# The opening norm of a two-block model: its inverse root alone on VectorE, its blocks scaled ahead of the shift, and the first mixer weights prepared between its blocks

## Chip, cores and metric

The kernel runs on one core of a Trainium2 chip. The metric is the device time of one execution in microseconds, the median over several runs. TensorE does the matmuls, VectorE (DVE in the views) and ScalarE (ACT) the elementwise work, GpSimd (POOL) some of it, and SyncE (SP) issues all the DMAs of weights and tables, in order.

## The reference

The input x is 256 tokens of 1024 features, all in float32. A first block of two layers is followed by a second block (gated linear attention, forgetting attention, cross-attention, a SwiGLU). Only the start of the first block matters here. In short:

```python
mod = (silu(c) @ ada_w[layer] + ada_b[layer])[:, None, :]
shift_m, scale_m, gate_m, shift_f, scale_f, gate_f = split(mod, 6)
h = rmsnorm(x, norm_g[layer, 0]) * (1.0 + scale_m) + shift_m
mix = mixer(h)                     # layer 0: convolution and retention; layer 1: S5
x = x + gate_m * mix
h = rmsnorm(x, norm_g[layer, 1]) * (1.0 + scale_f) + shift_f
x = x + gate_f * (square(relu(h @ w_fc1[layer])) @ w_fc2[layer])
```

The S5 mixer of layer 1 needs tables made from its parameters alone (complex exponentials and their powers, and per group of channels a matrix V and a matrix W). They don't depend on x, so the kernel makes them while the first layer runs.

## The kernel before

**Layout and weights.** Features lie on the partitions: x is eight blocks of 128 features by 256 tokens. Float32 is emulated: a weight piece of 1 MB (128 x 2048) is loaded by SP into a pool of four buffers, ScalarE makes its hi part (`hilo`, L314) and VectorE its lo part, the remainder (L315), in four quarters of 128x512. Each piece is then used in 48 matmuls of 128x256: hi by hi, hi by lo and lo by hi (`mm3`, L319 to L321). The activations are split into hi and lo as well.

**Modulation.** `ada(l, which)` makes 8 of a layer's 48 modulation columns: four pieces of 1 MB through the same four buffers, eight matmuls each (L439; the trace shows 16 records a piece), then a transposition on VectorE (L444) and the addition of the bias (L445). The first two calls make the scale and the shift of the first norm. All later ones are in a list (`Fill`) of which `step_piece` in the mixer takes some steps ahead of each weight piece (1.25 a piece on average).

**The norm.** `rms` squares x on ScalarE (L155), sums over the features on TensorE (L167), takes the inverse root on VectorE (`rsqrt`: eleven tiny operations, L344 to L349, behind L354) and spreads it over the partitions with TensorE (L369), into PSUM. `normed` then does for each of eight blocks: x times gain times root on VectorE (L397), the shift added on ScalarE, which gives hi (L398), and lo on VectorE (L399). The mixer's first weight pieces follow (`mixer0`, L497 on): value and gate of the convolution branch for j = 0 and 1 (`w_in` 0, 2, 1, 3), then tanh and the product (L518, L519), then the 31 taps of the convolution on VectorE, ScalarE and GpSimd.

**S5 preparation.** `s5_prep` (L739 to L835) is some 150 operations on VectorE and ScalarE (128x64 up to 128x576; complex products in `cmul`, L703 to L708). It is traced before the modulation. `s5_load(i)` loads the coefficients of group i (tile bc, L859), `s5_out(i)` makes the matrix V from them (L867, L871, L872, L881; for groups 0 to 2 on GpSimd), and `s5_tables` the rest: matmuls on V (L907), the matrix W on VectorE (L881, L921, L922), its transposition on TensorE (L928), copies on ScalarE (L929) and the stores to DRAM (Vd at L897, Wd at L932). `begin` starts groups 0 and 1 in the mixer; group 2 is started by `s5_tables` behind the first Wd store.

**Order.** The code is traced in one sequence; a scheduler then orders each engine's queue by a simulated time and a priority that falls with the place in the trace. `held(engines)` puts what is traced inside it behind the last instruction traced so far on these engines, `held_at(ends)` behind a given one, `later(n)` gives way to the next n instructions, and `after` puts steps of a fill behind an anchor on one engine. Each engine then works its queue strictly in that order.

## Time and profile before

| | |
|---|---|
| three runs | 1226.87, 1230.74, 1236.1 us |
| median | 1230.74 us |
| profiled execution, first to last instruction (span) | 1227.2 us |
| TensorE busy | 1169.7 us (95%) |
| VectorE busy | 891.7 us (73%) |
| ScalarE busy | 609.7 us (50%) |
| GpSimd busy | 106.1 us (9%) |

The span is measured from the first to the last instruction of one execution, and is what the profiled execution's own time is known by; it lies 0.3 us above the fastest run and 3.5 us below the median. TensorE is busy nearly everywhere, with two places of idle time in the first 210 us and one at 437 to 509 us. Times in the rows are microseconds from the span's start. Matmuls are pipelined, so the distance of two starts says what one costs, and its own duration is longer; the same holds for small operations of VectorE. The granted clock of TensorE (PEclk) is 1.00 at 2.4 GHz and 0.50 at 1.2 GHz.

### The profile page before, as it was taken

How to read it: one execution, taken by the hardware profiler on the slowest of the kernel's cores; microseconds unless marked ns; L12 is line 12 of the kernel's file. 1: busy time of each engine (PE TensorE's matmuls, PEld its weight loads, DVE VectorE, ACT ScalarE, POOL GpSimd, SP SyncE). 2: the span in 40 equal slices, each digit the busy share in tenths (PEclk: the TensorE clock that was granted, in tenths of full speed). 3: DMA queues.
4: the chain of work that ended last, by engine and by line, in shares of the span. 5: the costliest groups of instructions: out<-in, count | busy, mean ns of one | idle time of the engine just before them, and what ended most of it. 6: DMA issues, size and time to landing. Idle time of an engine off the chain costs nothing. (4 is left out here: it accounts for less than half of the span.)

```text
span 1227.2 us, 25417 instructions
## 1 busy us (share of the span) xinstructions
PE 1169.7 (95%) x10482; PEld 1109.3 (90%) x10482; DVE 891.7 (73%) x1821; ACT 609.7 (50%) x1202; POOL 106.1 (9%) x138
## 2 busy tenths in 40 slices
PE   6899897999999976899999999999999999999998
PEld 4698686999999964899999999999999999999998
DVE  7879888889888859767765656686667686665564
ACT  3577244655555542545544545573465545544441
POOL 0077321000000006200000000000000000000000
PEclk8899997999999977799999999999999999999999
DMA  9888886688888999554466655453443454555541
GB/s 341 340 311 327 297 294 212 238 265 282 297 287 267 300 249 309 216 172 171 169 243 212 233 174 172 164 172 104 151 159 138 172 168 148 194 179 177 194 155 60
DMA packets 69979, 267.29 MB, mean 218 GB/s; under 512 B 7380, under 2 KB 35428, under 8 KB 43240
## 3 DMA queue, kind: packets, MB, share of 16 engines
q1 hardware_dynamic: 69864, 265.68, 63.5%
q8 instruction: 82, 1.34, 0.4%
q14 instruction: 33, 0.27, 0.1%
HBM read 246.85 MB, written 18.81 MB: 216 GB/s over the span
## 5 line engine op out<-in xcount | busy, mean ns | idle before, releaser
L315 DVE TENSOR_TENSOR lo<-w,hi 128x512 fp32r<-128x512 f32 (+1 forms) x640 | 427.6, 712 | 147.7 <-ACT hi L314 147.1
L314 ACT ACTIVATE hi<-w 128x512 fp32r<-128x512 f32 (+1 forms) x640 | 358.4, 625 | 337.0 <-PE mm L320 118.8
L319 PE MATMUL mm<-h,hi 128*128 128x256 f32 x1328 | 379.7, 286 | 0.3 <-ACT h L398 0.3
L320 PE MATMUL mm<-h,hi 128*128 128x256 f32 x1328 | 377.7, 285 | 1.3 <-DVE h L399 1.1
L321 PE MATMUL mm<-h,lo 128*128 128x256 f32 x1328 | 378.6, 285 | 0.0
L319 PEld LDWEIGHTS mm<-h,hi 128*128 128x128 f32 x1328 | 254.7, 192 | 7.2 <-issue 3.4
L320 PEld LDWEIGHTS mm<-h,hi 128*128 128x128 f32 x1328 | 254.6, 192 | 2.8 <-DVE h L399 1.5
L321 PEld LDWEIGHTS mm<-h,lo 128*128 128x128 f32 x1328 | 254.5, 192 | 2.6 <-issue 1.6
L321 PE MATMUL at<-s,lo 128*128 128x256 f32 x720 | 204.4, 284 | 1.7 <-DVE lo L315 1.7
L319 PE MATMUL at<-s,hi 128*128 128x256 f32 x720 | 204.8, 284 | 0.0
L320 PE MATMUL at<-s,hi 128*128 128x256 f32 x720 | 204.1, 284 | 0.0
L321 PEld LDWEIGHTS at<-s,lo 128*128 128x128 f32 x720 | 137.9, 192 | 2.5 <-DVE lo L315 2.1
L319 PEld LDWEIGHTS at<-s,hi 128*128 128x128 f32 x720 | 138.0, 192 | 1.8 <-issue 1.4
L320 PEld LDWEIGHTS at<-s,hi 128*128 128x128 f32 x720 | 138.0, 192 | 0.6 <-issue 0.6
L439 PE MATMUL fa<-wa,crep 128*32 128x256 f32 x704 | 56.4, 428 | 7.0 <-DMA wa<-in_ada_dram 3.8
L537 POOL TENSOR_TENSOR s<-s,cv 128x256 f32<-128x256 f32 x60 | 49.9, 866 | 38.9 <-ACT cv L536 38.7
L439 PEld LDWEIGHTS fa<-wa,crep 128*32 128x32 f32 x704 | 23.0, 120 | 27.0 <-issue 6.4
L319 PE MATMUL fp<-h,hi 128*128 128x256 f32 x144 | 41.9, 291 | 0.7 <-ACT h L314 0.7
L320 PE MATMUL fp<-h,hi 128*128 128x256 f32 x144 | 41.8, 290 | 0.0
L321 PE MATMUL fp<-h,lo 128*128 128x256 f32 x144 | 41.6, 289 | 0.0
L929 ACT COPY Wt<-fp 128x512 f32<-128x512 f32 x32 | 18.6, 581 | 43.3 <-PE fp L928 39.9
L536 ACT ACTIVATE cv<-ap,s 128x256 f32<-128x256 f32 x60 | 29.5, 506 | 17.2 <-POOL s L537 16.4
(438 smaller groups left out, 1829.6 us busy)
## 6 DMA issues: line engine op xcount, KB each, us to landing
w<-in_fc_dram SPq DMA_DIRECT2D x64, 1024.0 KB, 5.1
wa<-in_ada_dram SPq DMA_DIRECT2D x44, 1024.0 KB, 6.5
w<-in_w_in_dram SPq DMA_DIRECT2D x38, 1024.0 KB, 4.9
w<-in_w_gate_dram SPq DMA_DIRECT2D x11, 1024.0 KB, 5.0
w<-in_w_up_dram SPq DMA_DIRECT2D x11, 1024.0 KB, 4.9
Vd<-V SPq DMA_DIRECT2D x16, 512.0 KB, 6.6
w<-in_w_out_dram SPq DMA_DIRECT2D x8, 1024.0 KB, 6.2
Wd<-Wt SPq DMA_DIRECT2D x16, 512.0 KB, 5.2
```

Of the source, the lines that this page charges most:

```text
L314: self.nc.scalar.activation(hi, h, AF.Copy)
L315: self.nc.vector.tensor_tensor(lo, h, hi.bitcast(F32), op=ALU.subtract)
L319: mm(ps, sh, mh, start=start, stop=False, skip_group_check=True)
L320: mm(ps, sh, ml, start=False, stop=False, skip_group_check=True)
L321: mm(ps, sl, mh, start=False, stop=stop, skip_group_check=True)
L439: nc.tensor.matmul(ps[32 * q:32 * q + 32], self.crep[:, 2 * k + k2], w[:, n:n + 256], start=k == 0 and k2 == 0, stop=k == 3 and k2 == 1, t ...
L536: nc.scalar.mul(t, src, w)
L537: nc.gpsimd.tensor_tensor(acc[:, ch], acc[:, ch], t, op=ALU.add)
L929: nc.scalar.copy(W[:, :, k], pt.rearrange("p (e x) -> p e x", e=4))
```

## The change

It has five parts.

1. The modulation is traced in front of most of the S5 preparation: the scale, three of the shift's four pieces, the root, then six of the eight blocks x times gain times root (`scaled`), and only then the shift's last piece, its transposition and addition. What is left of the S5 preparation is held behind the root on VectorE and gives way to the next 250 instructions. A `yield` of `s5_prep` moves so that the powers of the eigenvalues belong to that later part.
2. The first weight piece of the mixer (`w_in` 0) is loaded right behind the shift's pieces, and its four quarters are split between the blocks of the norm: `normed` calls the splitter behind every second block, held on VectorE and ScalarE.
3. `step_piece` returns that prepared piece at its first call, with no modulation step; at its second call the weights come first and the modulation's steps are put behind TensorE's last matmul; later calls are as before.
4. The gate's matmuls of j = 0 are held behind the value's on TensorE.
5. `s5_load` holds its DMA behind what SP was given last.

The number of instructions is the same on every engine. The diff, without removed comments (its line numbers are those of the changed kernel, 10 to 24 more than before):

```diff
+    def splitting(self, w, kn, n):
+        hi = self.wh.tile(...)
+        lo = self.wh.tile(...)
+        m = kn // 4
+        return (hi, lo), lambda q: self.hilo(hi[:, m * q:m * q + m], lo[:, m * q:m * q + m], w[:, m * q:m * q + m])
...
+    def scaled(self, x, r, g, c):
+        h = self.sb([128, T])
+        self.nc.vector.scalar_tensor_tensor(h, x[:, c], g[:, c:c + 1], r, op0=ALU.mult, op1=ALU.mult)
+        return h
+
+    def normed(self, x, r, g, shift, between=None, scaled=()):
         for c in range(8):
-            h = self.sb([128, T])
-            nc.vector.scalar_tensor_tensor(h, x[:, c], g[:, c:c + 1], r, op0=ALU.mult, op1=ALU.mult)
+            h = scaled[c] if c < len(scaled) else self.scaled(x, r, g, c)
             nc.scalar.activation(hh[:, c], h, AF.Identity, bias=shift[:, c:c + 1])
             nc.vector.scalar_tensor_tensor(hl[:, c], h, shift[:, c:c + 1], hh[:, c].bitcast(F32), op0=ALU.add, op1=ALU.subtract)
+            if between is not None and c % 2:
+                with self.held(mybir.EngineType.DVE, mybir.EngineType.Activation):
+                    between(c // 2)
...
         def step_piece(*a):
             self.np = getattr(self, "np", 0) + 1
-            if self.np > self.nofill:
+            if self.np > 2:
                 fill.step(self.rate)
-            return piece(*a)
+                return piece(*a)
+            if self.np == 2:
+                with self.held_at(self.norm_end):
+                    self.first = piece(*a)
+            if self.np == 2:
+                self.after(fill, self.rate, mybir.EngineType.PE, self.last(mybir.EngineType.PE))
+            return self.first
...
-            self.lin(pg, step_piece("w_in", 2 + j), h, K8)
+            with self.held(*() if j else (mybir.EngineType.PE,)):
+                self.lin(pg, step_piece("w_in", 2 + j), h, K8)
...
+        yield
         self.powers(PW, ab, 8, t)
-        yield
...
     def s5_load(self, i):
         bc = self.work([128, 4, 4, 16], "bc")
-        self.nc.sync.dma_start(...)
+        with self.held(mybir.EngineType.SP):
+            self.nc.sync.dma_start(...)
...
-            prep.drain()
+            prep.step(3)
+            Fill(self.ada(0, 1)).drain()
+            shift = Fill(self.ada(0, 0))
+            shift.step(3)
+            r = self.rms(x)
+            rms_dve = {DVE: self.last(DVE)}
+            gain = self.modg(0, 1, 0)
+            scaled = [self.scaled(x, r, gain, c) for c in range(6)]
+            with self.held(DVE):
+                shift.drain()
+            self.ada_end = {mybir.EngineType.SP: self.last(mybir.EngineType.SP)}
+            with self.held_at(rms_dve), self.later(250):
+                prep.step()
+            with self.held(DVE), self.later(250):
+                prep.drain()
...
-            Fill(self.ada(0, 1), self.ada(0, 0)).drain()
...
-                h = self.normed(x, self.rms(x), self.modg(0, 1, 0), self.modv(0, 0))
+                with self.held_at(self.ada_end):
+                    w = self.load(self.I["w_in"][0], 8, 256)
+                W, weigh = self.splitting(w, 8, 256)
+                h = self.normed(x, r, gain, self.modv(0, 0), weigh, scaled)
+                self.first = W
+                self.norm_end = {e: self.last(e) for e in (DVE, mybir.EngineType.Activation)}
+                self.norm_end.update(self.ada_end)
```

Three places show what becomes of the queues. The first is VectorE around the transposition of the shift's columns (STREAM_TRANSPOSE, from fa), before the change. The rows with 128x576 and 128x64 are S5 preparation, x with modg is a block's scaling.

```order
L816 TENSOR_TENSOR tiny_281<-tiny_281,early_283 128x576
L817 TENSOR_TENSOR tiny_281<-early_283,tiny_281 128x576
L704 TENSOR_TENSOR tw_231<-tiny_323 128x64
L705 TENSOR_TENSOR tiny_322<-tw_230,tw_231 128x64
L706 TENSOR_TENSOR tw_230<-tiny_322,tiny_323 128x64
L707 TENSOR_TENSOR tw_231<-tiny_323,tiny_322 128x64
L444 STREAM_TRANSPOSE s_452<-fa_411 128x256
L397 SCALAR_TENSOR_TENSOR s_510<-x,modg_506,at_503 128x256
```

The same place in the changed kernel, from the last of the six scaled blocks to the first quarter of lo.

```order
L400 SCALAR_TENSOR_TENSOR s_361<-x,modg_349,at_346 128x256
L729 TENSOR_TENSOR tw_230<-V_228,W_229 128x256
L730 TENSOR_TENSOR tw_231<-W_229,V_228 128x256
...
L458 STREAM_TRANSPOSE s_373<-fa_276 128x256
L400 SCALAR_TENSOR_TENSOR s_544<-x,modg_349,at_346 128x256
L731 TENSOR_TENSOR Wt_415<-early_416,early_417 128x576
L459 TENSOR_TENSOR mod_111<-s_373,vec 128x8
L400 SCALAR_TENSOR_TENSOR s_548<-x,modg_349,at_346 128x256
L410 SCALAR_TENSOR_TENSOR h_525<-s_351,mod_111,h_524 128x256
L410 SCALAR_TENSOR_TENSOR h_525<-s_353,mod_111,h_524 128x256
L533 TENSOR_SCALAR s_557<-vec 128x124
L322 TENSOR_TENSOR lo_523<-w_520,hi_522 128x512
```

Six scalings have moved ahead of the transposition, with ten operations of the S5 preparation between them and it, and the first quarter of the weights has moved between the blocks' subtractions. Between the root's first step and the transposition VectorE has 71 operations before and 58 now.

The second is VectorE at the second norm (ahead of the feed-forward part), from the first step of its root on, before the change. The rows L881 are table work for the third group, whose coefficients are bc_2225.

```order
L354 TENSOR_SCALAR s_2471<-at_2264 128x2
L881 TENSOR_TENSOR tw_2405<-bc_2225,tiny_280 128x512
L344 TENSOR_SCALAR s_2473<-s_2471 128x2
L346 SCALAR_TENSOR_TENSOR s_2474<-s_2471,s_2473 128x2
...
L397 SCALAR_TENSOR_TENSOR s_2520<-x,modg_2488,at_2485 128x256
L881 TENSOR_TENSOR W_2404<-sums_2228,tiny_280 128x512
L881 TENSOR_TENSOR W_2404<-bc_2225,tiny_280 128x512
L399 SCALAR_TENSOR_TENSOR h_2491<-s_2492,mod_111,h_2490 128x256
```

The same place in the changed kernel, where the third group's coefficients are bc_2205.

```order
L361 TENSOR_SCALAR s_2447<-at_2244 128x2
L905 TENSOR_TENSOR tw_2381<-bc_2205,tiny_424 128x512
L351 TENSOR_SCALAR s_2449<-s_2447 128x2
L353 SCALAR_TENSOR_TENSOR s_2450<-s_2447,s_2449 128x2
L905 TENSOR_TENSOR W_2380<-sums_2208,tiny_424 128x512
L905 TENSOR_TENSOR W_2380<-bc_2205,tiny_424 128x512
L354 TENSOR_TENSOR s_2450<-s_2450,s_2449 128x2
L945 TENSOR_TENSOR W_2380<-W_2380 128x512
L356 SCALAR_TENSOR_TENSOR s_2449<-s_2450,s_2449 128x2
L946 TENSOR_TENSOR W_2380<-W_2380,tw_2381 128x512
L353 SCALAR_TENSOR_TENSOR s_2450<-s_2447,s_2449 128x2
```

Four more of the table operations stand within the root, and the two between the scalings and the subtractions have gone from there.

The third is SP's queue. Before, the coefficients of groups 0, 1 and 2 are loaded in the opening, between the pieces of the first two modulations.

```order
L435 DMA wa_398<-in_ada_dram 128x2048
L859 DMA bc_1098<-in_bc_dram 128x256
L859 DMA bc_1109<-in_bc_dram 128x256
L859 DMA bc_2225<-in_bc_dram 128x256
L435 DMA wa_412<-in_ada_dram 128x2048
```

In the changed kernel groups 0 and 1 are loaded behind the mixer's fourth weight piece, and group 2 stands here, some 60 places further on, among the loads of the feed-forward part.

```order
L298 DMA w_2703<-in_fc_0_dram 128x2048
L921 DMA Vd_138<-V_1087 1024x1x128
L449 DMA wa_2768<-in_ada_dram 128x2048
L298 DMA w_2823<-in_fc_0_dram 128x2048
L956 DMA Wd_121<-Wt_2191 128x1024
L883 DMA bc_2205<-in_bc_dram 128x256
L298 DMA w_2902<-in_fc_0_dram 128x2048
```

The load of bc_2205 has moved behind the store of the first group's Wt.

## Rows read from the trace of the kernel before

**Rows 1.** Windows by stage: length, busy us of each engine (instructions), PEclk, DMA share, GB/s.

```profile
0.00:45.00 45.00, 27.49 (x205) 16.41 (x206) 35.20 (x160) 19.24 (x40) 2.34 (x17) 0.81 0.92 345
45.00:72.00 27.00, 27.00 (x266) 24.40 (x264) 16.20 (x36) 16.09 (x33) 10.02 (x13) 1.00 0.91 337
72.00:113.00 41.00, 41.00 (x373) 36.95 (x366) 39.42 (x70) 29.41 (x61) 32.50 (x38) 1.00 0.86 324
...
180.00:207.00 27.00, 18.71 (x166) 15.59 (x166) 25.24 (x49) 11.84 (x28) 7.87 (x6) 0.75 0.74 239
207.00:437.00 230.00, 229.08 (x2250) 217.00 (x2248) 194.30 (x325) 121.04 (x255) 0.17 (x2) 1.00 0.82 266
```

**Rows 2.** TensorE, timeline of the opening: start, us from first start to last end, count.

```profile
26.17 6.15 PE L439 MATMUL fa<-wa,crep 128*32 128x256 f32 x64
...
55.62 1.93 PE L439 MATMUL fa<-wa,crep 128*32 128x256 f32 x32
```

**Rows 3.** VectorE, timeline of the opening: start, us, operation.

```profile
17.84 0.16 DVE L354 TENSOR_SCALAR s<-at 128x2 f32<-128x2 f32 x1 [0.38 <-PE at L167]
...
29.73 0.75 DVE L707 TENSOR_TENSOR early<-W,early 128x576 f32<-128x576 f32 x1
30.40 0.21 DVE L705 TENSOR_TENSOR early<-early,early 128x64 f32<-128x64 f32 x1
30.54 0.75 DVE L708 TENSOR_TENSOR Wt<-early,early 128x576 f32<-128x576 f32 x1
...
34.94 0.44 DVE L444 STREAM_TRANSPOSE s<-fa 128x256 f32<-128x256 f32 x1
...
37.76 0.16 DVE L445 TENSOR_TENSOR mod<-s,vec 128x8 f32<-128x8 f32 x1
...
42.53 0.68 DVE L315 TENSOR_TENSOR lo<-w,hi 128x512 fp32r<-128x512 f32 x1
```

**Rows 4.** TensorE, timeline at 43.5 us: the first weight piece's third matmul, and later ones.

```profile
43.56 0.58 PE L321 MATMUL mm<-h,lo 128*128 128x256 f32 x1
...
44.16 0.41 PE L320 MATMUL mm<-h,hi 128*128 128x256 f32 x1
44.37 0.41 PE L321 MATMUL mm<-h,lo 128*128 128x256 f32 x1
```

**Rows 5.** Windows of TensorE alone: length, busy us (instructions), share, PEclk, DMA, GB/s.

```profile
34.70:44.90 10.20, 6.85 (x40) 0.50 0.88 355
46.00:55.00 9.00, 9.00 (x77) 1.00 0.87 325
```

**Rows 6.** VectorE, timeline of the second norm.

```profile
190.72 4.18 DVE L315 TENSOR_TENSOR lo<-w,hi 128x512 fp32r<-128x512 f32 x3
194.82 1.88 DVE L921 TENSOR_TENSOR W<-W 128x512 f32<-128x512 f32 x1
...
197.83 0.14 DVE L354 TENSOR_SCALAR s<-at 128x2 f32<-128x2 f32 x1
...
205.53 0.69 DVE L881 TENSOR_TENSOR W<-bc,tiny 128x512 f32<-128x512 f32 x1
206.13 3.25 DVE L399 SCALAR_TENSOR_TENSOR h<-s,mod,h 128x256 fp32r<-128x256 f32 x8
```

**Rows 7.** Weight loads of the first 45 us, from the view of tile w.

```profile
DMA to landing us min/median/max: 5.0/7.6/10.0
```

**Rows 8.** TensorE, timeline of the second norm: waits in brackets.

```profile
192.86 1.97 PE L907 MATMUL fp<-V,tiny 128*32 128x16 f32 x32 [2.40 <-ACT Wt L929]
194.75 1.87 PE L167 MATMUL at<-inv,q 128*128 128x1 f32 x8
...
206.67 0.38 PE L320 MATMUL mm<-h,hi 128*128 128x256 f32 x1 [1.13 <-DVE h L399]
```

**Rows 9.** GpSimd, timeline of the second norm: the last operation on a V matrix.

```profile
194.43 1.73 POOL L872 TENSOR_TENSOR V<-V,tv 128x576 f32<-128x576 f32 x1
```

**Rows 10.** Load of S5 coefficients at 190.66 us, from the view of tile bc.

```profile
DMA to landing us min/median/max: 7.2/7.2/7.2
```

8 lines of the change are left out of this document (5 added, 3 removed).

## Prediction, made before the changed kernel was run

> **What bounds the kernel now.** I read the table of windows first, one row for each stage [rows 1]. In the feed-forward part behind the first mixer (207 to 437 us) TensorE is busy for 229.08 of 230 us: there it sets the time, and every matmul that is moved into this stretch costs its full length. The stretches with something to gain are the opening (0 to 45 us: TensorE busy 27.49 us, DMA share 0.92, VectorE 35.20 us) and the second norm (180 to 207 us: TensorE 18.71 of 27 us, VectorE 25.24). Between them lies the convolution (72 to 113 us), with VectorE at 39.42 of 41 us; it starts when the mixer's opening matmuls have ended, so a lead won in the opening passes through it unshortened. The change reaches no further than the beginning of that feed-forward part: behind it the order of every engine is the same.
>
> In the opening the chain of the norm ends last. VectorE begins the inverse root at 17.84, mixed with the S5 parameters' preparation; TensorE has finished the shift's eight columns at 26.17 + 6.15 = 32.32, but VectorE transposes them at 34.94 and adds the bias at 37.76, two microseconds and many operations behind [rows 2, 3]. Only then can ScalarE and VectorE make the first block of h. The third matmul of the first weight piece waits for its lo part (42.53 + 0.68) and runs at 43.56 [rows 3, 4]. From 34.7 to 44.9 the granted clock is 0.50 (1.2 GHz, TensorE busy 6.85 of 10.2 us), and from 46 us 1.00 [rows 5].
>
> **The change, part by part.** *Opening, up to the shift.* The order shows 71 operations of VectorE between the inverse root's start and the shift's transposition, 58 in the changed kernel. 18 operations of 128x64 and three of 128x576 leave the stretch; six scaled blocks enter it, and the root's eleven steps stand alone. At the spacing of the rows (0.67 us from 29.73 to 30.40, 0.14 to 30.54) [rows 3] 18 x 0.14 + 3 x 0.67 = 4.5 us leave. Six blocks at 3.25 / 8 = 0.40 us (the row at 206.13, the same form) [rows 6] bring 2.4. The root's eleven steps, which each wait for the one before, cost at least 0.14 each (the row of its first at 197.83) [rows 6], where other operations filled these waits; I estimate 1.4 us for it. 34.94 - 4.5 + 2.4 + 1.4 is 34.2; I take 34.3, between TensorE's end at 32.4 and today's 34.94. Behind the transposition stand one scaled block and one 128x576 operation, then the addition: 34.3 + 0.37 + 0.40 + 0.67 + 0.1 = 35.9, against 37.8 now.
>
> *First weight piece.* VectorE now runs two blocks' subtraction and then a quarter of the weights. First block on ScalarE 0.5, then two subtractions at 0.4, one small operation 0.14, one lo of 0.6: lo is there at 38.0, so the third matmul comes 5.5 us earlier than 43.56. The piece needs 48 matmuls. Before, they ended at 55.62 - 48 x 0.12 = 49.86, since the second piece runs without a gap ahead of the modulation's matmuls at 55.62 [rows 2, 5]; that is 6.3 us behind the third matmul, 1.3 of them at the half clock. After, the cover of the two modulation pieces that TensorE had in its wait is gone, so the piece may start at the half clock for longer: I give it 7.0 us and its end 45.0, a lead of 4.9 us. The bounds: 43.8 if it runs at full clock, held by the pace of VectorE alone (two subtractions and one lo, 1.45 us a quarter, 5.8 in all), so 6.1; 47.5 if all 48 run at 0.20 (the pitch at half clock, 44.16 to 44.37) [rows 4], so 2.4. The first weights' load stands one place earlier on SP's queue than now, where a modulation piece stood, and takes 7.6 us to land, 10.0 at most [rows 7]. I take it as in time, since TensorE no longer waits for a late root before the matmuls that free its buffer; where it is late, the lead shrinks toward 2.4.
>
> *Two modulation pieces later.* The mixer's first two weight pieces bring no modulation piece along until the second is in, so 24 of these pieces lie ahead of the second norm and not 26. The two run in the saturated feed-forward part. Two pieces at full clock take 1.93 us (the row at 55.62, 32 records) [rows 2]: +1.9.
>
> *The S5 preparation*, held back by up to 250 instructions, goes into VectorE's gaps at 45 to 72 us and costs nothing as long as it ends before the convolution's work fills VectorE at 72 us. Its rest is some 60 small operations, 10 us, in 27 us of which VectorE is idle for 10.8 (27.00 - 16.20) [rows 1]: some of them run there already, so the cover is enough, and what overflows would cost its own length.
>
> *Second norm.* Here the order changes without the text of the norm changing. The load of the third group's S5 coefficients (bc_2205) was in the opening and now stands behind a store on SP's queue; the table work on VectorE has moved with it. Before: one table operation inside the root, two between the scaling and the subtraction, two more behind. After: five inside the root and none between. The root starts at 197.83, behind a 1.88 us operation and others [rows 6], though TensorE's sums for it ended at 194.75 + 1.87 = 196.62 [rows 8]. In the changed kernel those operations stand ahead of the last residual; the start can move to 196.6, which is -1.2. If the sums themselves come earlier, because TensorE no longer waits 2.4 us at 192.86 [rows 8], it is -3.6; if not at all, 0. Four more table operations inside the root cost 0.60 each when free (the spacing from 205.53 to 206.13) [rows 6], 2.4 us; beside GpSimd they cost up to 1.75 each, 7.0 us. That price is in the rows: from 190.72 to 196.16 GpSimd builds a V matrix, its last operation at 194.43, and three lo operations take 4.18 us and the next 1.88, while the same kinds take 0.68 when GpSimd is idle [rows 6, 9]. I take the middle, 4.7, as GpSimd's six operations on the third V matrix now start when the coefficients land, which is about when the root begins. The two table operations between scaling and subtraction go: -1.2. Together -1.2 + 4.7 - 1.2 = +2.3, between -2.4 and +7.0 (the upper end with 0 for the start, 7.0 for the tables, the same -1.2, and 1.2 for a wait on the coefficients).
>
> The Trainium skill, page "SBUF — State Buffer", section "Who interferes with whom", says that a VectorE instruction with two inputs in SBUF contends with a GpSimd instruction that reads SBUF, and that the holder keeps the shared ports for the whole instruction. The trace agrees (0.68 against 1.4 to 1.9 us). It speaks against this change: where GpSimd works throughout, the term stands at its upper end, which is the second rival below.
>
> **The sum**: -4.9 + 1.9 + 2.3 = -0.7 us. It is made against an execution with a span of 1227.2 us, which lies 3.5 below the median of the runs shown (1230.74) and close to the fastest (1226.87); taken off the median it gives 1230.0 us.
>
> **Rivals.** *First: the lead arrives whole and the tables run free.* For it speaks that GpSimd's second matrix is through early, and that the coefficients may land only when the root is over. Then -6.1 + 1.9 - 1.2 + 2.4 - 1.2 = -4.2, so 1226.5, and with an end at -3.6 for the start 1224.1.
>
> *Second: GpSimd works through the whole root.* Then all four added table operations cost 1.75 us, the start is where it was, and 1.2 are lost on the way to the coefficients: -4.9 + 1.9 + 7.0 = +4.0, so 1234.7. For it speaks that all six operations on the third V matrix are now behind the landing, where before two had been done early; against it, that 1.75 is the price of a 128x512 operation that meets a GpSimd operation at its start, and only one in a row can. That is what the rule of the page "SBUF — State Buffer" in the Trainium skill would give.
>
> *Third, slower: the late coefficients hold the second norm.* The place: the second of the root's operations on VectorE is followed in its queue by a table operation that reads bc_2205, and TensorE's queue has 16 matmuls on the third V matrix ahead of the feed-forward part's first. SP issues the load only behind the store of the first Wt. If that store goes no earlier than the matmuls of before at 192.86, which waited for the same copy of Wt, and the load takes 7.2 us [rows 8, 10], it lands at 200.1. GpSimd then needs its seven operations at some 1.6 (1.73 for the long ones) [rows 9], so 211.3, and TensorE 1.97 for its matmuls: 213.3 against the 206.67 at which the feed-forward part runs freely now [rows 8]. That is +6.6 there, and in all -4.9 + 1.9 + 6.6 = +3.6, so 1234.3. It decides once the coefficients land behind about 196; every microsecond behind costs one, and over 1% slower (12.3 us) needs a landing at 209. Against it: TensorE now has the first Wt's transpositions in the middle of the last output piece and not behind it, so the store should go some 5 us earlier.
>
> *Fourth: the change doesn't do what it says.* Ten operations of the preparation still lie between the scaled blocks and the shift's transposition, and TensorE, with no work in its wait, keeps the low clock through the first piece: lead 2.4 only. Then -2.4 + 1.9 + 2.3 = +1.8, 1232.5.
>
> **How the numbers follow.** The forecast (within about 3 us of 1230.0) has 0.46, the free tables 0.22, GpSimd through the root 0.08, the late coefficients 0.13, the lead that stays away 0.11. A range from 1223.5 (6.1 + 2.4 gained, 1.9 paid) to 1237.5 (2.4 gained, 1.9 and 7.0 paid) holds them all but their tails, about 8 in 10. One per cent, 12.3 us, is about what a measurement of this kernel tells from no change (its three runs spread over 9.2 us). None of the cases reaches it: faster by over 1% would need the second norm's idle 8.3 us of TensorE to go as well as the whole lead, 0.06; slower by over 1% needs the coefficients at 209 or an overflow of the preparation into the convolution, 0.06; within 1%: 0.88.
>
> **What would show it.** Right: the shift's addition near 35.9, the third matmul near 38, the first piece's end near 45, two modulation pieces fewer before the second norm, five table operations within the root, the root's end not earlier than now by more than a microsecond or two after the lead is taken off. Wrong: an end of the first piece earlier than 43.8 or later than 47.5; VectorE full before 72 us; a gap of TensorE ahead of the matmuls on the third V matrix; a granted clock below 1.00 behind 46 us in the mixer, which no term here holds.

## The result, and the profile after

| | before | after |
|---|---|---|
| median, us | 1231.59 (1226.87 to 1236.1, four runs) | 1247.86 (1244.66 to 1249.52, four runs) |
| ratio to before, 95% interval | | 1.0133 [1.0109, 1.0156] |
| span of the profiled execution, us | 1227.2 | 1247.1 |

The changed kernel is slower by 1.3%. The prediction said 1230.0 us and at most 1237.5: its sign, its range and its likeliest case are wrong. The spans lie further apart (19.9 us) than the medians (16.3). In after the span is 1.8 us shorter than the time of the same execution (1247.1 and 1248.87); so the profiled execution of before took about 1229.0 us, an estimate, which is 1.7 below the median of its three runs and not 3.5. "After" below is the changed kernel, whose lines are numbered some 7 to 24 higher than in before (L319 is L326, L439 is L453, L537 is L560).

The stages of after, in a table of windows with the columns of [rows 1]; the last two rows are the first feed-forward part, shifted with it, and the S5 mixer behind it. The row alone is that mixer in before:

```profile
45.00:72.00 27.00, 23.07 (x218) 20.50 (x217) 24.33 (x60) 15.96 (x33) 12.66 (x15) 0.96 0.82 307
...
215.00:446.00 231.00, 230.92 (x2259) 217.37 (x2262) 192.13 (x320) 121.22 (x254) 0.17 (x2) 1.00 0.80 263
446.00:523.00 77.00, 47.25 (x740) 35.90 (x732) 54.87 (x98) 24.81 (x44) 25.17 (x38) 0.73 0.98 261
```

```profile
437.00:509.00 72.00, 50.15 (x751) 39.75 (x751) 59.60 (x111) 28.59 (x52) 25.11 (x38) 0.69 0.97 284
```

Against [rows 1], TensorE lost 3.9 us of work in 45 to 72 us, where it had been full, and VectorE is busy for 24.33 us there and not 16.20. The feed-forward part is as full as it was. The mixer behind it is new to the story: TensorE is busy for 47 of 77 us there, and for 50 of 72 us in before.

To place the loss I took seven marks of TensorE's timeline in each kernel. This table (worked out from the records, not a view) gives for before the time in us, for all others the distance to it in their profiled executions. Where nothing differs upstream, marks still differ by 1 to 2 us from one execution to another, so single entries say no more than that. "Flows" is the first matmul of the feed-forward part that the next one follows within 0.3 us; where the granted clock is 0.50 there, as in after, it is one matmul, 0.4 us, later than in before. The profiled executions of a_powlate and best2_7 are the shortest of theirs, 8 and 6 us below the medians, so their rows flatter them; those of best3, a_order and a_rate44 are the longest, 3 to 4 us above.

| kernel | first mixer piece | first output piece | last output matmul | feed-forward flows | its last matmul | gated unit | end |
|---|---|---|---|---|---|---|---|
| before | 41.8 | 151.7 | 187.6 | 206.7 | 434.6 | 501.9 | 1227.2 |
| after | -4.9 | +4.2 | +5.6 | +7.6 | +8.7 | +21.2 | +19.9 |
| b_hold | -1.8 | +2.1 | -0.3 | +1.2 | +4.2 | +14.8 | +15.8 |
| b_hold_fix | -2.6 | +2.2 | -0.1 | +1.5 | +5.1 | +11.1 | +11.6 |
| a_nohold | -4.3 | -0.8 | -1.2 | -0.5 | 0.0 | +13.0 | +14.3 |
| a_powlate | -4.3 | +0.2 | +1.6 | +3.6 | +3.5 | +6.9 | +5.6 |
| a_nohold_powlate | -4.2 | -2.1 | -1.2 | -0.5 | -0.2 | +11.7 | +10.3 |
| b_nofill | -2.6 | +3.1 | +9.8 | +7.4 | +8.0 | +19.6 | +18.4 |
| a_two | -5.0 | +8.4 | +7.3 | +11.3 | +12.4 | +15.5 | +16.5 |
| a_fills7 | -3.4 | +9.0 | +8.1 | +4.7 | +7.8 | +21.0 | +19.2 |
| a_rate44 | -3.5 | +3.3 | +5.4 | +7.8 | +10.1 | +14.2 | +14.2 |
| a_nohold_rate44 | -4.4 | +1.6 | +1.2 | +2.0 | +7.4 | +5.5 | +6.5 |
| b_bad | +0.5 | +0.6 | -0.1 | +0.3 | +1.4 | +3.6 | +4.1 |
| a_order | -4.3 | +2.5 | +5.2 | +8.4 | +9.8 | +17.4 | +18.8 |
| best1 | -4.9 | -2.1 | -2.5 | -1.8 | +3.6 | +1.7 | +2.6 |
| best2_7 | -5.0 | +1.4 | +2.3 | -3.2 | -1.8 | +7.1 | +5.3 |
| best2_7_fix | -4.5 | +1.6 | +2.4 | -2.6 | -0.6 | +2.8 | +3.3 |
| best3 | -4.6 | +4.5 | +7.3 | +0.2 | +1.7 | +10.7 | +11.7 |

The row of after reads: 4.9 us won in the opening; 9.1 lost between there and the output pieces; 3.4 more up to the feed-forward part; 1.1 in it; 12.5 in the S5 mixer, where the prediction looked for nothing.

The marks do not stand behind the same work in all kernels, and so a lead can look larger than it is. By the records of fa (16 a modulation piece) TensorE has done 10 pieces ahead of the first mixer piece in before and 8 in after; by the end of the fourth mixer piece it is 13 and 11, at the first output piece 29 and 27. Two pieces cost 1.93 us [rows 2], so of a lead at the same mark that much is work put off. At the first output piece the kernels with two pieces put off are after, a_nohold, a_powlate, a_nohold_powlate, b_nofill, a_rate44, a_nohold_rate44, a_order and best1.

**The opening.** VectorE's timeline of after (start, us, operation), then TensorE's, then a window of TensorE alone:

```profile
34.41 0.16 DVE L459 TENSOR_TENSOR mod<-s,vec 128x8 f32<-128x8 f32 x1
```

```profile
37.71 0.58 PE L328 MATMUL mm<-h,lo 128*128 128x256 f32 x1
...
45.37 0.28 PE L328 MATMUL mm<-h,lo 128*128 128x256 f32 x1
```

```profile
34.70:42.70 8.00, 5.72 (x25) 0.50 0.50 209
42.70:55.00 12.30, 12.30 (x126) 1.00 0.88 320
```

The shift is added at 34.41 (forecast 35.9), the third matmul comes at 37.71 (38.0), and the first piece ends at 45.37 + 0.28 = 45.65 (45.0). It runs at the half clock up to 42.7. In before the same piece ends with this matmul, at 49.93:

```profile
49.65 0.28 PE L321 MATMUL mm<-h,lo 128*128 128x256 f32 x1
```

So the lead at the first piece's end is 4.3 us, and 2.4 without the two pieces put off.

**The start of the convolution.** VectorE, GpSimd, ScalarE and TensorE of after, timelines (GpSimd's first row is the first tap alone, the second the first seven together), then a window of TensorE behind its wait:

```profile
58.76 0.28 DVE L728 TENSOR_TENSOR tiny<-tw,tw 128x128 f32<-128x128 f32 x1
59.07 0.71 DVE L729 TENSOR_TENSOR tw<-tiny,tiny 128x128 f32<-128x128 f32 x1
...
64.73 0.99 DVE L730 TENSOR_TENSOR tw<-tiny,tiny 128x256 f32<-128x256 f32 x1
...
67.17 0.22 DVE L728 TENSOR_TENSOR tiny<-tw,tw 128x64 f32<-128x64 f32 x1
67.43 0.75 DVE L729 TENSOR_TENSOR tw<-tiny,tiny 128x64 f32<-128x64 f32 x1
```

```profile
56.88 2.75 POOL L560 TENSOR_TENSOR s<-s,cv 128x256 f32<-128x256 f32 x1 [4.17 <-ACT cv L559]
...
56.88 7.64 POOL L560 TENSOR_TENSOR s<-s,cv 128x256 f32<-128x256 f32 x7 [4.17 <-ACT cv L559]
```

```profile
59.67 0.51 ACT L559 ACTIVATE cv<-ap,s 128x256 f32<-128x256 f32 x1 [2.47 <-POOL s L560]
...
66.64 0.24 ACT L755 COPY tiny<-tiny 128x64 f32<-128x64 f32 x1 [1.57 <-DVE tiny L731]
...
67.59 2.17 ACT L321 ACTIVATE hi<-w 128x512 fp32r<-128x512 f32 x4
...
70.47 0.57 ACT L541 ACTIVATE s<-mm 128x512 f32<-128x512 f32 x1
```

```profile
71.10 0.58 PE L326 MATMUL mm<-h,hi 128*128 128x256 f32 x1 [3.93 <-ACT s L541]
71.48 0.42 PE L327 MATMUL mm<-h,hi 128*128 128x256 f32 x1
71.69 0.42 PE L328 MATMUL mm<-h,lo 128*128 128x256 f32 x1
...
75.45 1.71 PE L453 MATMUL fa<-wa,crep 128*32 128x256 f32 x16
77.10 0.39 PE L327 MATMUL mm<-h,hi 128*128 128x256 f32 x1
```

```profile
71.00:74.80 3.80, 3.70 (x17) 0.50 0.55 164
```

And GpSimd's taps in the same stretch of before:

```profile
57.72 2.15 POOL L537 TENSOR_TENSOR s<-s,cv 128x256 f32<-128x256 f32 x3 [24.38 <-ACT cv L536]
```

The chain goes through four queues. The postponed S5 preparation runs at 57 to 69 us, among the convolution's first taps on GpSimd, which in before meet no preparation there. The first tap begins at 56.88 in the middle of VectorE's run (quarters of lo and operations of the preparation) and takes 2.75 us; seven take 7.64 / 7 = 1.09 each, against 2.15 / 3 = 0.72 before. From 59.07 the two engines take turns: the preparation's operations of 128x128 and 128x256 take 0.71 to 0.99, where the one at 58.76 took 0.28, and one of 128x64 takes 0.22 at 67.17, while GpSimd waits, and 0.75 at 67.43 beside its next tap. ScalarE's next tap activation waits 2.47 us for a tap, and a copy that belongs to the preparation itself (L755) waits 1.57 us for VectorE; behind them in ScalarE's queue stand the split of the fifth weight piece and the tanh that frees the product buffer. TensorE waits 3.93 us for that tanh. Then it has the half clock: its matmuls start 0.21 us apart, and 19 of them with 16 of the modulation take 77.10 - 71.10 = 6.0 us, where 19 x 0.12 + 1.07 = 3.35 was the pace before the wait. Wait and clock together, 3.9 + 2.7 = 6.6 us, are more than the lead of 4.3 that TensorE still had at the fourth piece's end. The preparation does not do this alone: without the hold on the coefficients the wait is 1.5 us and the clock stays up, with the preparation in the same stretch (a_nohold, below).

The Trainium skill, page "SBUF — State Buffer", section "Who interferes with whom", says that a VectorE instruction with two SBUF inputs and a GpSimd instruction that reads SBUF exclude each other for a whole instruction. The trace agrees: 0.71 us against 0.28 for VectorE's 128x128, 1.09 against 0.72 for GpSimd's tap.

**The second norm.** VectorE, GpSimd and TensorE of after, then VectorE in a_nohold (below), where GpSimd is idle at that point:

```profile
197.28 0.16 DVE L361 TENSOR_SCALAR s<-at 128x2 f32<-128x2 f32 x1 [0.46 <-PE at L167]
...
199.75 1.13 DVE L353 SCALAR_TENSOR_TENSOR s<-s,s 128x2 f32<-128x2 f32 x1
...
204.71 1.35 DVE L356 SCALAR_TENSOR_TENSOR s<-s,s 128x2 f32<-128x2 f32 x1
...
208.75 0.16 DVE L356 SCALAR_TENSOR_TENSOR s<-s,s 128x2 f32<-128x2 f32 x1
```

```profile
198.72 0.97 POOL L891 TENSOR_TENSOR sums<-bc 128x128 f32<-128x128 f32 x1 [13.15 <-DMA bc<-in_bc_dram]
...
206.12 1.80 POOL L896 TENSOR_TENSOR V<-V,tv 128x576 f32<-128x576 f32 x1
```

```profile
208.96 1.22 PE L376 MATMUL at<-ident,s 128*128 128x128 f32 x4 [9.18 <-DVE s L356]
```

```profile
195.96 0.16 DVE L353 SCALAR_TENSOR_TENSOR s<-s,s 128x2 f32<-128x2 f32 x1
```

The root's last step on VectorE in before:

```profile
200.31 0.16 DVE L349 SCALAR_TENSOR_TENSOR s<-s,s 128x2 f32<-128x2 f32 x1
```

The third group's coefficients land late, and GpSimd works from 198.72 to 207.92, through the whole inverse root. Four operations on 128x2 numbers take 1.13 to 1.35 us there, where GpSimd's instructions take 1.21 to 1.80, and 0.16 as soon as GpSimd is through. Of the five table operations inside the root one takes 1.70 us and the others 0.68 or 0.69. From its first step to the end of its last the root takes 208.91 - 197.28 = 11.6 us, in before 200.47 - 197.83 = 2.6 [rows 6].

**The S5 mixer.** It works on eight pairs of groups. For each, `load` brings a table Wt, for every second pair the rows Mt in eight small transfers, and a table Vt, all on SP's queue; TensorE multiplies by Wt, ScalarE copies, TensorE transposes, VectorE scans, GpSimd combines, TensorE multiplies by Mt and Vt. The scans of before start at 457.0, 461.8, 467.3 and so on, 5 us apart; those of after at 467.4, then 482.7, 488.2 and on. SP's queue of after and of before, TensorE of after (timelines), and TensorE's waits at 440 to 480 us, of after and of before (line, what it waited for: us in total, times, longest):

```profile
423.27 0.39 SPq L449 DMA_DIRECT2D wa<-in_ada_dram  x1
...
427.88 0.33 SPq L449 DMA_DIRECT2D wa<-in_ada_dram  x1
429.91 1.62 SPq L1025 DMA_DIRECT2D Wt<-Wd  x2
435.44 9.19 SPq L1043 DMA_DIRECT2D Mt<-Kd  x8
...
446.67 9.71 SPq L1043 DMA_DIRECT2D Mt<-Kd  x8
...
458.12 1.22 SPq L1025 DMA_DIRECT2D Wt<-Wd  x2
...
464.49 4.99 SPq L1025 DMA_DIRECT2D Wt<-Wd  x4
```

```profile
415.29 1.65 SPq L1001 DMA_DIRECT2D Wt<-Wd  x2
...
429.90 1.16 SPq L1001 DMA_DIRECT2D Wt<-Wd  x2
431.64 8.24 SPq L1019 DMA_DIRECT2D Mt<-Kd  x8
```

```profile
443.60 0.63 PE L453 MATMUL fa<-wa,crep 128*32 128x256 f32 x4
...
445.14 1.92 PE L453 MATMUL fa<-wa,crep 128*32 128x256 f32 x28
...
475.46 1.08 PE L1061 MATMUL mm<-Wt,s 128*32 128x128 f32 x16 [10.47 <-DMA Wt<-Wd]
```

```profile
PE mm L1061 <- DMA Wt<-Wd: 10.8, 2, 10.5
```

```profile
PE mm L1037 <- DMA Wt<-Wd: 1.2, 2, 0.9
```

Two modulation pieces are loaded at 423.27 and 427.88 and used at 443.60 and 445.14, behind the feed-forward part. They are the two that the opening no longer takes. In the feed-forward part itself stand ten modulation pieces in before and in after: it takes a fixed number along. The two hold two of the weight buffers, which the tables of the second, third and fourth pair share, and stand on SP's queue ahead of the mixer's Wt and Mt. The third pair's table, which before loads at 429.90, ahead of the second group of rows, stands behind both groups in after, in the four loads at 464.49 (the two at 458.12 are the fifth pair's, which goes to another pool), and TensorE waits 10.5 us for it.

### The profile page after: what moved, and what is told of

It is laid out like the page before. It is cut to its first block, busy times and chain, and to the rows that moved or that the text cites. A ratio compares the mean times of both kernels' runs of the same rounds, so it can differ in the third digit from the quotient of the medians.

```text
span 1247.1 us, 25412 instructions
## 1 busy us (share of the span) xinstructions
PE 1174.5 (94%) x10482; PEld 1112.4 (89%) x10482; DVE 901.2 (72%) x1821; ACT 610.0 (49%) x1202; POOL 110.6 (9%) x138
## 5 line engine op out<-in xcount | busy, mean ns | idle before, releaser
L326 PE MATMUL mm<-h,hi 128*128 128x256 f32 x1328 | 382.1, 288 | 8.3 <-ACT hi L321 4.4
L326 PEld LDWEIGHTS mm<-h,hi 128*128 128x128 f32 x1328 | 257.0, 194 | 16.6 <-ACT hi L321 5.3
L326 PE MATMUL at<-s,hi 128*128 128x256 f32 x720 | 204.7, 285 | 0.0
L326 PEld LDWEIGHTS at<-s,hi 128*128 128x128 f32 x720 | 138.0, 192 | 2.3 <-issue 1.8
L453 PE MATMUL fa<-wa,crep 128*32 128x256 f32 x704 | 56.2, 418 | 5.4 <-DMA wa<-in_ada_dram 4.9
L560 POOL TENSOR_TENSOR s<-s,cv 128x256 f32<-128x256 f32 x60 | 53.5, 927 | 17.1 <-ACT cv L559 16.9
L453 PEld LDWEIGHTS fa<-wa,crep 128*32 128x32 f32 x704 | 22.0, 116 | 24.6 <-DMA wa<-in_ada_dram 7.0
L326 PE MATMUL fp<-h,hi 128*128 128x256 f32 x144 | 41.0, 285 | 0.9 <-ACT h L321 0.9
L559 ACT ACTIVATE cv<-ap,s 128x256 f32<-128x256 f32 x60 | 29.4, 505 | 17.8 <-POOL s L560 17.7
```

The source lines that it names most:

```text
L326: mm(ps, sh, mh, start=start, stop=False, skip_group_check=True)
L453: nc.tensor.matmul(ps[32 * q:32 * q + 32], self.crep[:, 2 * k + k2], w[:, n:n + 256], start=k == 0 and k2 == 0, stop=k == 3 and k2 == 1, t ...
L559: nc.scalar.mul(t, src, w)
L560: nc.gpsimd.tensor_tensor(acc[:, ch], acc[:, ch], t, op=ALU.add)
```

## The experiments

Every kernel computes the whole output. Kernels named a_ and best start from after, those named b_ from before. Ratios are to the kernel before on the same chip, with 95% intervals.

**One part alone.** Only the first mixer's first weight piece without its modulation steps:

```
-        self.defer, self.conv_sw, self.nofill = 4, True, 0
+        self.defer, self.conv_sw, self.nofill = 4, True, 1
```

> The kernel before, with one thing of the change: the mixer's first weight piece takes no modulation step along, so all later modulation pieces come later and the list's last two 1 MB pieces are loaded at the end of the first feed-forward part, ahead of the S5 mixer's tables. Theory A (these two late pieces take the loads of the S5 mixer's W matrices out of their order): the S5 mixer shows a wait of TensorE for Wt of about 10 us, as in the changed kernel (before 1.2), and the whole is 10 to 14 us slower than before, ratio about 1.010. Theory B (the loss comes from the new opening and the second norm): no such wait, within 3 us of before.

Measured: 1247.11 us, 1.0124 [1.0087, 1.0161]. This flag alone costs as much as the whole change, and mostly in the same place: 11.6 of its 18.4 us are lost in the S5 mixer. Its scans start at 466.3 and 483.1, the stall of after.

Only the hold on the coefficients' load:

```
-        self.nc.sync.dma_start(bc...)
+        with self.held(mybir.EngineType.SP):
+            self.nc.sync.dma_start(bc...)
```

> The kernel before with the hold on the load of the S5 coefficients as its only change. Theory C: 4 to 5 us slower than before, lost between the second norm and the feed-forward part, with the opening and the S5 mixer unchanged. Theory D: within 2 us of before.

Measured: 1244.25 us, 1.0106 [1.0078, 1.0134]. That is more than either theory had. It loses 10.6 us in the mixer too, but elsewhere: the first seven scans keep their pace and the eighth comes 15.9 us behind the seventh. ScalarE's and TensorE's waits of this kernel at 480 to 520 us:

```profile
ACT hi L314 <- DMA w<-in_glu_a_dram: 12.2, 1, 12.2
```

```profile
PE at L1044 <- ACT s L1040: 11.1, 2, 9.9
```

In ScalarE's queue the split of the gated unit's first weights, whose transfer has not landed, stands ahead of the copy that the last scan needs. b_hold_fix is b_hold with that split held behind the copy:

```
+            copied = self.last(mybir.EngineType.Activation)
-            scanned = {mybir.EngineType.DVE: self.last(mybir.EngineType.DVE)}
+            scanned = {mybir.EngineType.DVE: self.last(mybir.EngineType.DVE), mybir.EngineType.Activation: copied}
```

> The kernel before with the hold on the mixer's coefficient preparation alone, as in b_hold, and with ScalarE's splits of the gated unit's weights held behind the copy that the mixer's last scan needs. If the 10.6 us that b_hold lost inside the S5 mixer are an accident of ScalarE's queue (the split that waits for its transfer stands ahead of the copy), the stall between the seventh and the eighth scan goes, the mixer loses under 2 us, and the kernel stands at about 4 us over before (1234 to 1237), which is the hold's own price ahead of the mixer. If the hold itself delays the mixer, the loss of about 10 us stays (1243 to 1246).

Measured: 1238.63 us, 1.005 [1.0032, 1.0068]. The eighth scan is back at 4.8 us behind the seventh, so that stall was the split's place in the queue. But the mixer still loses 6.0 us, not under 2: TensorE now waits 6.3 us for the last rows Mt, 3.2 in before. So the hold costs about 5 us up to the end of the feed-forward part and some 6 in the mixer; the rest of b_hold was an accident of the order on ScalarE.

**One part taken back.** After without the hold:

> The changed kernel without the hold on the load of the S5 coefficients, which are then loaded in the opening again. Theory C (the 4 to 5 us lost between the second norm's start and the feed-forward part come from the third group's late coefficients): the offset against before at the feed-forward part falls from 8.5 to about 4, and the whole is 4 to 5 us faster than the changed kernel, about 1243. Theory D (they come from the order of the table work and the tensor queue alone): no change, 1248.

Measured: 1242.16 us, 1.0088 [1.0066, 1.0109]. The feed-forward part flows at -0.5 and not +7.6, so ahead of the S5 mixer the hold carries most of the loss. In the mixer nothing changes: 13.0 us lost, the second scan 15.9 us behind the first. Of the 8.1 us 5.0 are won back by the first output piece, so most of the hold's price in after lies ahead of the second norm. At the fifth piece TensorE waits 1.5 us, where after waits 3.93, and the granted clock stays at 1.00, though the postponed preparation still runs, at 54 to 68 us:

```profile
PE mm L326 <- ACT s L541: 1.5, 1, 1.5
```

In a_fills7, a_rate44 and a_order, which keep the hold and the preparation, that wait is 3.92 or 3.93 us again; a_two, which takes three more modulation pieces ahead of the fifth piece, has none. How the hold lengthens it is not shown; VectorE begins the operations of 128x128 at 57.75 in after and at 53.81 here.

After with twice the modulation steps at the first mixer's second weight piece, so that no piece is left over:

```
-                self.after(fill, self.rate, mybir.EngineType.PE, ...)
+                self.after(fill, 2 * self.rate, mybir.EngineType.PE, ...)
```

> The changed kernel, with twice the modulation steps at the mixer's second weight piece, so that the count of pieces is again that of before from there on. Theory A: the S5 mixer's W loads stand as before on SP's queue, TensorE waits less than 2 us for them (10.5 in the changed kernel), and the time falls by 10 to 13 us to about 1236. Theory B: it stays within 3 us of the changed kernel's 1248.

Measured: 1244.0 us, 1.0101 [1.0079, 1.0123]. The S5 mixer loses 3.1 us and not 12.5, but the first mixer, where the steps now lie, loses 4.2 more (output pieces at +8.4), 1.9 of it the two pieces' own matmuls. The time falls by 3.9 us and not by 10 to 13. Two steps more at the retention (fills 5 to 7), with the same aim:

> The changed kernel, with seven instead of five modulation pieces used between the retention's matmuls and the convolution's layer norm, where TensorE has idle time; so no piece is left for the end of the first feed-forward part. Theory A2 (the two pieces at that end, by their 2 MB and by the weight buffers that the S5 mixer's W loads take over from them, cost the S5 mixer 10 to 12 us): the stretch from the feed-forward part's last matmul to the S5 mixer's gated output falls from 12.5 us above before to less than 4, the whole by 7 to 11 us to 1237 to 1241. Theory H (the S5 mixer's loss comes from the hold on the coefficients, which the kernel before with the hold alone lost there too): loss stays above 9, whole 1245 or more.

Measured: 1246.5 us, 1.0119 [1.0101, 1.0137], a miss: the two pieces are gone from the S5 mixer, and the other stall is there (the eighth scan 17.8 us behind the seventh, with ScalarE's split waiting 13.2 us for the gated unit's weights, as in b_hold).

After with more modulation steps in the feed-forward part, and the same without the hold:

```
-        self.rates = (1.25, 0.375, (0, 0, 0), 0.25, (0, 0))
+        self.rates = (1.25, 0.4375, (0, 0, 0), 0.25, (0, 0))
```

> The changed kernel, with 0.4375 instead of 0.375 modulation pieces a step in the first feed-forward part as its only change, so that the two pieces run in its middle. Theory A2: loss in the S5 mixer below 4 us, the feed-forward part 2 us longer, whole 1237 to 1241. Theory H: loss in the S5 mixer stays above 9, whole 1248.

> The changed kernel without the hold on the coefficients' load, and with a rate of 0.4375 instead of 0.375 modulation pieces a step in the first feed-forward part, so that the two postponed pieces are used in its middle and not at its end. Theory A: the S5 mixer's loss falls from 13 us (without the hold alone) to less than 4, whole 1231 to 1236. Theory E: loss in the S5 mixer unchanged, whole about 1244.

Measured: a_rate44 1240.12 us, 1.0069 [1.0053, 1.0086]; a_nohold_rate44 1236.54, 1.0042 [1.0025, 1.006]. With the two pieces inside the feed-forward part the mixer's loss falls from 12.5 to 4.1 us, and without the hold it becomes a gain of 1.9. The pieces' price is then paid in the full stretch: 2.3 us with the hold, 5.4 without, where the prediction had 1.9; what makes the second so much dearer is not shown.

**The preparation's collision.** The last 24 of VectorE's postponed operations (the powers) put where they are first used instead, in the code of the rotations, where they run at 408 to 423 us, late in the first feed-forward part:

```
-        self.powers(e8, u, 8, t)
+        self.u8 = u
...
-        self.powers(e4, [e8[k][:, 8] for k in range(2)], 2, t)
...
+        self.powers(e8, self.u8, 8, t)
+        self.powers(e4, [e8[k][:, 8] for k in range(2)], 2, t)
```

> The changed kernel, with the last 24 VectorE operations of the S5 preparation (two sets of powers for the rotations) moved to where they are first used, late in the first feed-forward part, where VectorE has room. Theory F (the postponed preparation collides with GpSimd's taps at the start of the convolution and eats the opening's lead): the fifth weight piece keeps the lead, its offset against before goes from +2 to about -4, GpSimd's first taps take 0.72 us each and not 1.09, and the time falls by 3 to 6 us. Theory G (the lead is lost because the next weights' loads or the convolution's own chain set the time): the fifth piece stays within 2 us of the changed kernel.

Measured: 1242.46 us, 1.0091 [1.0069, 1.0114]; its runs spread from 1234.6 to 1247.1, and the profiled one (span 1232.8) is the shortest, so the last two marks in its row flatter it. GpSimd's first eleven taps take 8.04 / 11 = 0.73 us each, TensorE's wait at the fifth piece falls from 3.93 to 1.58 us and the clock stays at full level:

```profile
68.77 0.39 PE L326 MATMUL mm<-h,hi 128*128 128x256 f32 x1 [1.58 <-ACT s L541]
```

The output pieces begin at +0.2 and not at +4.2. Both causes together, no hold and the powers late:

> The changed kernel without the hold and with the powers prepared at the start of the mixer's turns; modulation rates as in the change. If the opening's lead of 4.3 us is lost only to the preparation's collision in the convolution and to the hold, it stands through the convolution and the first feed-forward part (last product of that part about 4 us ahead of before), the S5 mixer loses 3.5 us or less to the two late modulation pieces, and the time is 1228 to 1232. If the lead is lost to something else as well, the feed-forward part begins no earlier than in before, and the time is 1234 to 1240.

Measured: 1239.66 us, 1.0066 [1.0045, 1.0087], by its expectation the case "lost to something else as well". There is no wait left at the fifth piece. The output pieces begin at -2.1, of which 1.9 are the two pieces put off: of the 4.2 us at the first mark (2.3 without them) little is left there, and 0.5 at the feed-forward part. And the mixer loses 11.9 us although its second scan follows the first at 4.9 us: TensorE waits for W tables later on, and for the last rows Mt, which the profile names by the load that follows them on the queue:

```profile
PE at L1104 <- DMA m<-in_mem_dram: 10.0, 1, 10.0
PE mm L1062 <- DMA Wt<-Wd: 8.2, 5, 4.1
```

**The order on SP.** In before, the third and fourth pair's tables put behind the first three rows of the third group, as after's queue has it (an instruction order alone, no pieces moved):

```
+            if ip in (2, 3):
+                late.extend(SP's loads of this pair's Wt)
...
+                    if ip == 4 and s == 2:
+                        (every load in late goes behind the last one traced on SP)
```

> The kernel before, with nothing changed but the place of four loads on SP's queue in the S5 mixer: the W matrices of groups 4 to 7 (two 1 MB tiles) stand behind the first three loads of the third Kd matrix, as they do in the changed kernel. Theory A (the place of these loads costs the S5 mixer its time): offset against before 0 up to the S5 mixer, there 8 to 12 us with a wait of TensorE for Wt of about 10 us, whole about 1241. Theory E (it is the two late modulation pieces' own 2 MB on the DMA engines, 5 us, or the lateness of everything before): within 3 us of before.

Measured: 1233.04 us, 1.0006 [0.9991, 1.0021]: the order alone, with the loads as early as in before, costs nothing that shows. The reverse, after with the pairs' tables back in their order (the second group of rows then stands behind two more Vt tables and one more Wt table than in before, so this is not before's queue exactly):

```
+                with self.held_at({SP: self.wl[3]} if ip == 4 else {}):
+                    Wt = wide("Wt", self.wplace[ip], ip)
+                self.wl = {..., ip: self.last(SP)}
...
+                with self.held_at({SP: self.wl[ip]} if ip in (2, 4) else {}):
                     for s in range(8): (loads of Mt)
```

> The changed kernel, with SP's loads of the S5 mixer put back into the order of before (the third and fourth pair's first tables ahead of the rows of the sums that the change lets pass them). If the mixer's loss of 12.5 us is the order that the two late modulation pieces bring about on SP's queue (the third pair's table behind 9 us of other loads), the stall of 15 us between the first and the second scan goes, the mixer loses under 5 us and the kernel stands at 1236 to 1241. If the loss is the two pieces themselves (their buffers and their 3.4 us of TensorE ahead of the mixer), the order changes nothing and it stays at 1244 to 1249.

Measured: 1244.61 us, 1.0106 [1.0085, 1.0128]. The stall behind the first scan goes (468.0, then 472.8), as the order's theory wants, but the mixer still loses 7.6 us and the time is the other theory's. SP's loads for the mixer stand later than in before, the first Wt by 16 us (415.29 in before) and the second group of rows by 22 (431.64), as this timeline of SP in a_order shows:

```profile
431.32 0.84 SPq L1025 DMA_DIRECT2D Wt<-Wd  x2
...
453.48 10.92 SPq L1047 DMA_DIRECT2D Mt<-Kd  x8
```

So the single long stall needs the order and the lateness together; with the order mended the lateness comes out in smaller waits. The order mended without the hold, where the loads are less late (a_nohold's first Wt stands at 421.41), was not run.

**Looking for a better kernel.** No hold, rate 0.4375, powers late:

> The three remedies together in the changed kernel: no hold on the coefficients, the two pieces in the middle of the feed-forward part, the last powers late. If theories A, C and F hold, the opening's lead of 4 us reaches the end: 1226 to 1230, at or below before's 1231. If one is wrong: 1235 or more.

Measured: 1233.42 us, 1.0007 [0.9989, 1.0025]. The same with seven fills in place of the rate, then with ScalarE's split held behind the last scan's copy:

> The changed kernel without the hold on the coefficients, with the last powers of the S5 preparation late, and with the two pieces at the retention instead of in the feed-forward part. If the opening's lead of about 4 us survives to the feed-forward part and the S5 mixer keeps before's pace: 1226 to 1229, 2 to 5 us below before. If the lead is paid back at the retention or in the second norm: 1231 or more.

> The changed kernel without the hold, with the powers prepared at the start of the mixer's turns and seven modulation fills (as best2_7), and with ScalarE's splits of the gated unit's weights behind the copy that the last scan needs. By the theory that best2_7's loss inside the S5 mixer (8.9 us) is that same accident: the stall of the eighth scan goes, and the time is 1228 to 1232. If the loss has another cause, it stays at about 1240.

Measured: best2_7 1240.19 us, 1.0075 [1.0048, 1.0102]; best2_7_fix 1232.41 us, 1.0007 [0.9991, 1.0023]. The split alone was worth 7.8 us between the two by the medians, and its stall (the eighth scan 13.2 us behind the seventh) is gone. Last, best2_7_fix with the rows Mt ahead of the later tables on SP, as in before:

> As best2_7_fix (no hold, powers late, seven modulation fills, ScalarE's splits behind the last scan's copy), with the loads of the sums' rows ahead of the later pairs' tables on SP, as before has them. best2_7_fix has these rows 7 us later than before, its last outputs wait 4.6 us for their rows and its mixer loses 3.4 us. If that is the order on SP, the mixer loses 1 us or less and the time is 1227 to 1230; if not, it stays at about 1232.

Measured: 1236.98 us, 1.0042 [1.0026, 1.0059], a miss: the order of before is worse here, because two Vt loads that wait for a buffer then stand ahead of the first rows (11.08 us for four issues at 419.5). No version beat the kernel before.

## Why the prediction was wrong

- **Opening (right).** "a lead of 4.9 us" at the first piece's end, bounds 2.4 to 6.1: 4.3 there and at the fourth piece's end (the 4.9 in the table is the first matmul). The half clock in the first piece was inside the bounds given. As the sum had it, 1.9 of the lead is work put off.
- **"A lead won in the opening passes through it unshortened" (the first step that failed).** I read the convolution as one full engine, VectorE [rows 1], and did not follow ScalarE's and GpSimd's queues at its start, where [rows 1] shows GpSimd busy for 10.02 of 27 us. At the fifth piece TensorE waited 3.93 us for a tanh in ScalarE's queue.
- **"The S5 preparation ... costs nothing as long as it ends before the convolution's work" (failed, mis-sized).** It ended in time, at 69 us. I counted VectorE's idle time and operations at their free price, and left out that each one that meets a GpSimd tap lengthens both. The same collision that I had priced for the second norm was not priced here. Together with the hold it took 6.6 us from TensorE at the fifth piece, 2.7 of them by the clock, which the prediction named as a sign against it. Either one taken back leaves about 1.5 us of waiting and the full clock (a_powlate 1.58, a_nohold 1.5), both taken back none. A part of the hold in this stretch stood in no term.
- **"+1.9" for two modulation pieces in the feed-forward part (failed).** That part has ten before and ten after; the two ran behind it, at 443.60 to 447. I assumed that what the list has left over spreads itself out, where a fixed rate decides.
- **Second norm, "+2.3" (size right by luck, working wrong).** From the last output matmul to the flow it became 2.0 us longer in after, 1.6 between the same matmuls. But the root became 9.0 us longer, where I gave the tables in it 4.7 and 7.0 at most, and it began 6.1 us earlier behind the last output matmul (4.0 us, in before 10.2), where I gave 1.2 and 3.6 at most; the two misses cancel. I charged the collision to the table operations; the small operations of the root paid most of it, 1.13 to 1.35 us in place of 0.16. That is the second rival's place (GpSimd through the whole root), with the late landing of the third (1.25 us of the root are a wait for the coefficients). What the hold costs in all was taken too low: without it, the feed-forward part flows 8.1 us earlier (a_nohold), 1.3 of this within the norm.
- **"Behind it the order of every engine is the same" (the step that cost most).** 12.5 of the 19.9 us were lost behind it. The text of that part is the same; its inputs are not: two more weight pieces in the shared buffers, SP's queue with them ahead of the mixer's loads, and a schedule drawn anew from there. b_nofill brings the loss about by one flag; a_rate44 and a_nohold_rate44, with the pieces used earlier, bring it down to 4.1 and below zero.
- **The chances.** All four rivals stayed within 7 us of before, since each varied a term that I had already named. None let the change act where its text does not. The range's ends also don't come out of the terms given for them, which make 1224.1 and 1237.2; it alters nothing.

By medians, taking back the hold and placing the two pieces in the feed-forward part brings the 1247.86 us to 1236.54 (a_nohold_rate44), and the powers' place to 1233.42 (best1), where nothing is left that a measurement can tell from before. So these three together remove the slowdown; the split of it between them is not additive, as a_nohold_powlate and the wait at the fifth piece show.

What stays open: where the lead without the work put off (2.3 us at the first matmul) goes ahead of the output pieces when hold and collision are gone; why a_nohold_powlate loses 11.9 us in the mixer and a_powlate, with the same order on SP, 3.4 in its profiled execution, its shortest; how the hold lengthens the wait at the fifth piece; and why best2_7_fix, which has its two pieces behind it and still 2.6 us at the feed-forward part, gives them back by the mixer's end.

## What to carry to other kernels

Work that is moved "into the gaps" of one engine has to be checked against what the other engines do in those gaps, above all GpSimd beside VectorE, and against the in-order queues behind them: here slow taps and a copy of the moved work itself held a tanh on ScalarE, and that held TensorE. A lead should be measured where the same work has been done: two modulation pieces put off looked like 1.9 us won. Work that is no longer done early must be followed to where it is done: a fill at a fixed rate doesn't take it up, and what is left over lands at the next border between stages, with its buffers and its place on the load queue. Where a scheduler draws the order, "unchanged code" is no reason to call a stage unchanged; compare the queue of loads there before giving it a zero.

## What the runs showed of the hardware that was not expected

VectorE operations that met GpSimd instructions here took close to the length of those, however small they were: 1.13 to 1.35 us for 128x2 numbers that take 0.16 alone, beside GpSimd's 1.21 to 1.80, and 0.71 to 0.99 for the preparation's 128x128 and 128x256, beside taps of 1.09 on average. So the smallest were hit hardest, relative to their own price. And a wait of TensorE of 3.93 us in a full stretch was followed by 1.2 GHz (granted clock 0.50) from 71.10 to about 77, where the pace is again that of before the wait, which cost 2.7 us more, where a wait of 1.58 us at the same place (a_powlate) was followed by the full level.
